# Hybrid recurrence and pooling block: sums of the heads' outputs made by accumulating stores, pool products moved into the ring of weight blocks

## The chip, the cores and the metric

The kernel runs on one core of a Trainium2 chip. The core has a matrix engine (TensorE, PE in the profile, with its weight loads PEld), a vector engine (VectorE, DVE), a scalar engine (ScalarE, ACT), GpSimd (POOL) and a sync engine (SyncE, SP) that here does nothing but issue DMAs. Work memory is SBUF; matmuls write to the banks of PSUM, of 128 x 512 float32 each. Tensors "in DRAM" are in the chip's memory. Each engine takes its instructions strictly in order, and so does each DMA queue's issuer: an instruction that waits holds all behind it on its engine.

The metric is device time in microseconds (us). Before: a median of 1468.33 us over three runs (1466.95 to 1468.78). Beside them stands one profiled execution, from which the rows shown come.

## What is computed

A decoder block over 1024 tokens of width 1024, in float32. Shortened from the reference:

```python
proj = x @ w_in
q, f_pre, i_val, o_gate, pool_v, gate_a, gate_b = jnp.split(proj, splits, axis=-1)
o = hgrn2_chunked(qf, 1 - f, i_val, log(f))          # 8 heads of 128, a gated recurrence over the tokens
o = o * lax.rsqrt(jnp.mean(jnp.square(o), axis=-1, keepdims=True) + RMS_EPS)
o = o.reshape(B, S, hw) * hgrn_norm_g * jax.nn.sigmoid(o_gate)
a = o @ w_a
pooled = causal_multiscale_pool(pool_v)              # trailing means over 2, 4, 8, 16 tokens, minus the token
b = jnp.einsum('bsgc,gcd->bsgd', pooled, w_pool).reshape(B, S, POOL_WIDTH) * pool_scale
mix = (jax.nn.sigmoid(gate_a) * a + jax.nn.sigmoid(gate_b) * b) @ w_out
x = layer_norm(DEEPNORM_ALPHA * x + mix, ln1_g, ln1_b)
x = layer_norm(DEEPNORM_ALPHA * x + jnp.square(jax.nn.relu(x @ w_up)) @ w_down, ln2_g, ln2_b)
```

## The kernel before

**Products.** A float32 matrix product is made of three passes over parts: each operand is split in a high part (an ACT cast, L118 or L123) and a low part (a DVE subtract of source and high part, L119 or L124), and the matmuls take high x high, high x low, low x high. On top of that the large products go by a scheme with seven instead of eight block products. The tokens are the halves u = 0 and 1, the inner dimension is cut in halves as well, and `pair` (L256) makes two column tiles at once: the blocks b11, b12, b21, b22 of the weight are combined by DVE (L273 and the lines of `t4`, L277 to L279), split, and multiplied as P1, P2, P7, P4, P6, P5, P3, in that order, with the token operands a11, a12, s3, a22, s2, s1, s4. Each P is 12 matmuls of 128 x 512 (`prod`, L201 to L204). P1 is copied out of its PSUM bank by ACT (L264), P2 and the others are added by DVE (L268). A pair uses three banks, "a", "c" and "z"; P7 opens "z". A bank comes from the ring of four "pj" or from another tag (w_a's pairs take "hg" and "sc" for "z").

**Rings.** Weight blocks of 256 KB are loaded into "raw" tiles, a ring of six (`block_tile`), in order by SP. Their parts go to "w", a ring of ten tiles, that is five pairs of high and low. Temporary rows lie in "c" (four and two tiles), and in the head stage in q, f (three each), og, v (two each) and others (`tt`, L613).

**Stages.** The values of all heads come first (to about 70 us). Then come eight heads, each in two halves of 512 tokens (`hgrn`, L786): `head_inputs` makes the head's q and f, POOL does small work on the ends of subblocks (L799 on), PE and DVE the recurrence, ACT the squares (L903), a square root (L904) and the scaling (L908), PE turns the result (L911), and DVE multiplies it by the norm's gain and by the gate in the tile og (L912). L913 stores og to `od[h][u]`. The og tile was loaded with the head's gate through `loaded` (L574), on SP.

What is put between the halves as filling is listed in `EXTRAS` (L917 on): `pooled` (w_in's columns for pooling, and the trailing means, stored to `po`), `gates` (w_in's columns of both gates; the gate of b is stored to `gb`), `o_sums`, and `pool_products`.

`o_sums(kp)` (L585) loads the outputs of head kp and head kp+4 in both halves from `od` (four loads), makes the operands s3, s2, s1 and s4 of w_a's seven products with four DVE operations (L588 to L591) and stores them to `osd` (four stores). It runs for kp = 0 to 3, three times as filling and once right after the last half, in tiles tC to tF. `o_operand` loads a11, a12 and a22 from `od`, and s1 to s4 from `osd`, when w_a's pairs need them, and splits them.

`pool_products(g)` loads w_pool's block of group g into a raw tile and splits it, loads the pooled tiles from `po`, splits them, makes four results of six matmuls each (L105 to L107 are the three passes), scales and gates them with `gb` (L709) and stores them to `pb`. All of the parts of w_pool, the pooled tiles and the results come in rotation from the rooms q, f, og and v, twelve in all, so that a room is used again while a store from it may still be under way.

After this come w_a's four pairs (`a_pair`, L981), which add the pooled branch from `pb`, then w_out, the first layer norm, w_up and w_down.

**Order.** The order of instructions on each engine is not the order of the program text: a scheduler sorts them at build time with a timeline of its own (`schedule_with_timeline_sim`), bounded by priorities. So an edit in one place can move instructions elsewhere. PE's order is the same in both kernels up to the sixth head (about 515 us in the profile) and again from the later part of w_a on; in between it differs. The number of matmuls is the same.

Of the kernel before, what the change touches and what calls it, by code (L numbers as in the profile page):

```python
# [9 lines left out]
F32 = mybir.dt.float32  # L10
F32R = mybir.dt.float32r
U32 = mybir.dt.uint32
AF = mybir.ActivationFunctionType
ALU = mybir.AluOpType

_TC = dict(schedule_with_timeline_sim=True)
P = 128
# [4 lines left out]
HEADS = 8  # L22
HALF = 512
CH = HALF // P
# [19 lines left out]
def tile_hybrid_block(  # L44
# [46 lines left out]
    def ps_tile(tag="pj", bufs=4):  # L91
        if tag == "hg":
            hg_tags.append(hg_tags.pop(0))
            tag, bufs = hg_tags[-1], 1
        return pp.tile([P, HALF], F32, tag=tag, name=nm("ps_" + tag), bufs=bufs)
# [20 lines left out]
    def split(src, tile_of):  # L116
        hi, lo = tile_of(), tile_of()
        A.copy(hi, src)  # L118
        V.tensor_sub(lo, src, f(hi))  # L119
        return hi, lo  # L120
# [48 lines left out]

    xt = [[None] * CH for _ in range(3)]  # L170

    def first_tokens(name, *tags):
        for kp in range(CH):
            ps, _ = transposed(r[:CH], HALF if name == "a12" else 0, kp, tags[kp % len(tags)])
            in_parts(name, kp, ps)
            A.copy(xt[name == "a12"][kp], ps)
# [29 lines left out]
    def block_tile(shape=(CH, P)):  # L206
        return wq.tile([P, *shape], F32, tag="raw", name=nm("raw"), bufs=6)
# [45 lines left out]
    def c_late():  # L253
        return c_tile(False)

    def pair(raw, rooms, takes, pz_tag="pj", pc_tag="pj"):  # L256


        b11, b12, b21, b22, t = raw if len(raw) == 5 else (*raw, None)
        c, ps = {}, {}  # L260

        def copied(room, ps):
            t = room()
            A.copy(t, ps)  # L264
            return t

        def added(t, ps):
            V.tensor_add(t, t, ps)  # L268
            return t

        def t3():
            c["t"] = block_tile() if t is None else t
            V.tensor_sub(c["t"], b22, b12)  # L273
            return w_part(c["t"])

        def t4():
            V.tensor_sub(b12, b12, b11)  # L277
            V.tensor_sub(c["t"], b22, b12)
            V.tensor_sub(b21, b21, c["t"])  # L279
            return w_part(b21)  # L280

        def t2():
            return w_part(c["t"])

        def t1():
            return w_part(b12)

        def p1(w):
            ps["a"] = ps_tile()
            prod(ps["a"], w, "a11", True)  # L290
            c[11] = copied(rooms[0], ps["a"])

        def p2(w):
            ps["c"] = ps_tile(pc_tag, 4 if pc_tag == "pj" else 2)
            prod(ps["c"], w, "a12", True)

        def p7(w):
            ps["z"] = ps_tile(pz_tag, 4 if pz_tag == "pj" else 2)
            prod(ps["z"], w, "s3", True)
            with tc.high_priority(PRIO):  # L300
                takes[0](added(c[11], ps["c"]))
                c[22] = copied(rooms[2], ps["z"])

        def p6(w):
            prod(ps["a"], w, "s2", False)
            with tc.high_priority(PRIO):
                c[21] = copied(rooms[1], ps["a"])
                takes[2](added(c[21], ps["z"]))

        def p4(w):  # L310
            prod(ps["z"], w, "a22", False)

        def p5(w):
            prod(ps["a"], w, "s1", False)
            with tc.high_priority(PRIO):
                takes[3](added(c[22], ps["a"]))

        def p3(w):
            prod(ps["a"], w, "s4", False)
            with tc.high_priority(PRIO):  # L320
                takes[1](ps["a"])

        def t0():
            return w_part(b11)

        def b_21():
            return w_part(b21)

        def b_22():
            return w_part(b22)  # L330

        return tuple(
            ((operand,), ((operand, product),))
            for operand, product in ((t0, p1), (b_21, p2), (t3, p7), (t4, p4), (t2, p6), (t1, p5), (b_22, p3))
        )

# [45 lines left out]
    with tc.tile_pool(name="xr", bufs=8, side="right", reuse_waits="tile") as xr:  # L382
# [9 lines left out]
        PE.transpose(ps[:, 0:32], prm_r, ident[0:32, 0:32])  # L392
        V.tensor_copy(prm, ps[:, 0:32])
        g_col, pscale = prm[:, 16:24], prm[:, 24:32]
        lb = const.tile([P, 8], F32, name="lb")
        one_lb = const.tile([P, 8], F32, name="one_lb")
        e01 = const.tile([P, 16], F32, name="e01")
# [174 lines left out]
    def loaded(src, tile_of):  # L572
        t = tile_of()
        nc.sync.dma_start(out=t, in_=src)  # L574
        return t
# [6 lines left out]
            xp[name][kp] = act_tile()  # L582
            split_into(xp[name][kp], loaded(src, c_tile))

    def o_sums(kp, tile_of=c_tile):  # L585

        a11, a21, a12, a22 = (loaded(od[k][u], tile_of) for k, u in ((kp, 0), (kp, 1), (kp + CH, 0), (kp + CH, 1)))
        V.tensor_add(a22, a21, a22)  # L588
        V.tensor_sub(a21, a11, a21)
        V.tensor_sub(a11, a22, a11)  # L590
        V.tensor_sub(a12, a12, a11)  # L591
        for name, t in zip(("s3", "s2", "s1", "s4"), (a21, a11, a22, a12)):
            nc.sync.dma_start(out=osd[name][kp], in_=t)

    hg_scope = ExitStack()
    hgp = hg_scope.enter_context(tc.tile_pool(name="hgp", bufs=1, reuse_waits="tile"))
    mg_scope = ExitStack()
    with tc.tile_pool(name="tmp", bufs=1, side="right", reuse_waits="tile") as tmp:
# [14 lines left out]
        def tt(tag, dtype=F32):  # L613
            pool = tmp if tag in ("q", "f", "og", "v") else hgp
            return pool.tile([P, HALF], dtype, tag=tag, name=nm(tag), bufs=RINGS.get(tag, 1))
# [71 lines left out]

        def pool_products(g):

            tags = iter(("q", "f", "og", "v") * 3)  # L690

            def room(dtype=F32):
                return tt(next(tags), dtype)

            raw = block_tile((2, 2 * P))
            nc.sync.dma_start(out=raw, in_=w_pool[g].rearrange("(k p) c -> p k c", p=P))
            wh, wl = split(raw, lambda: room(F32R).rearrange("p (k c) -> p k c", c=2 * P))
            for u in range(2):
                pl = [split(loaded(pod[2 * g + i][u], room), row_tile) for i in range(2)]
                for i in range(2):  # L700
                    w = slice(i * P, (i + 1) * P)
                    j = 2 * g + i
                    t = room() if j == KT - 1 else loaded(gbd[j][u], room)
                    ps = ps_tile()
                    mm3(ps, [(wh[:, c, w], wl[:, c, w], *pl[c]) for c in range(2)])
                    if j == KT - 1:
                        A.activation(t, ps, AF.Copy, scale=pscale[:, j : j + 1])
                    else:
                        V.scalar_tensor_tensor(t, ps, pscale[:, j : j + 1], t, ALU.mult, ALU.mult)  # L709
                    nc.sync.dma_start(out=pbd[j][u], in_=t)  # L710
# [75 lines left out]
        def hgrn(h, u, ft, q, v, og, state):  # L786
# [122 lines left out]
            pt = ps_tile("tr", 2)  # L909
            for c in range(CH):  # L910
                PE.transpose(pt[:, c * P : (c + 1) * P], on[:, c * P : (c + 1) * P], ident)  # L911
            V.scalar_tensor_tensor(og, pt, g_col[:, h : h + 1], og, ALU.mult, ALU.mult)  # L912
            nc.sync.dma_start(out=od[h][u], in_=og)  # L913
            return st


        EXTRAS = {(h, 1): (("pooled", h),) for h in range(4)}  # L917
        EXTRAS[4, 1] = (("gates", 0),)
        EXTRAS[5, 1] = ("gates", 1), ("o_sums", 0)
        EXTRAS[6, 1] = ("gates", 2), ("o_sums", 1)  # L920
        EXTRAS[7, 0] = (("gates", 3),)
        EXTRAS[7, 1] = (
            ("gates", 4), ("o_sums", 2), ("pool_products", 0), ("gates", 5), ("pool_products", 1), ("gates", 6), ("pool_products", 2), ("pool_products", 3), ("gates", 7),
        )
        nxt = head_inputs(0, (None, None, "p6", None, None, None, None))
        output_gates(0)
        for h in range(HEADS):
            fs, qs = nxt
            state = None
            for u in range(2):  # L930
                v, og = values(h, u), loaded(ogd[h][u], lambda: tt("og"))
                with tc.high_priority(PRIO_LAST) if (h, u) == (HEADS - 1, 1) else nullcontext():
                    state = hgrn(h, u, fs[u], qs[u], v, og, state)
                    if (h, u) == (HEADS - 1, 1):
                        tags = iter(("tD", "tE", "tF", "tC"))
                        o_sums(h - CH, lambda: tt(next(tags)))
                if h + 1 < HEADS and u:
                    nxt = head_inputs(h + 1)
                    if h % 2:
                        output_gates(h + 1)  # L940
                for what, j in EXTRAS.get((h, u), ()):
                    dict(gates=gates, pooled=pooled, pool_products=pool_products, o_sums=o_sums)[what](j)


        hg_scope.close()
# [34 lines left out]

        def a_pair(p):  # L981
            cols = 2 * p * P, (2 * p + 1) * P
            raw = loaded_blocks(w_a, *cols) if p % 2 else wide_blocks(w_a, cols[0], mg_raw)
            room = mg_tile("room", 4)
            takes = [gated(2 * p + i, u, p < 2) for u in range(2) for i in range(2)]
            return pair(raw, (c_tile, room, room), takes, "hg")

        def unpark(*which):
            for u, j in which:
# [388 lines left out]
```

## Time and profile before

| | us |
|---|---|
| median of three runs | 1468.33 |
| lowest and highest | 1466.95, 1468.78 |
| profiled execution, time | 1467.26 |
| profiled execution, span in the trace | 1465.5 |
| PE busy | 1441.2 |
| DVE busy | 1137.4 |
| ACT busy | 756.8 |
| mean granted clock of TensorE | 0.996 |

How to read the rows that follow in the prediction. A row of the groups has a line of the kernel, its engine and operation, what it writes and reads, the count, then busy time and the mean of one in ns, then idle time just before them with what ended it. A row of the timeline begins with start and duration in us, and has in brackets the idle time before and its releaser. A row of the stretches has from and to, the length, then busy time and count for PE, PEld, DVE, ACT and POOL, the granted clock, the DMA engines' busy share and GB/s. A row of the waits says which engine and line waited for which: total us, times, the longest. A row of the DMA issues has the count, KB each, and the median us from issue to landing. "SPq" and "POOLq" are the queues that these engines issue. L1269 is the line of a load that POOL issues late in the kernel.

### The profile page before, as it was taken

To read this page: it belongs to the slowest core of one execution; us is meant where nothing else is said; L and a number is where in the kernel's file an instruction comes from. 1 tells how busy PE (TensorE), PEld (TensorE's weight loads), DVE (VectorE), ACT (ScalarE), POOL (GpSimd) and SP (SyncE) were. 2 spreads that over 40 slices of the span, in tenths; PEclk is the share of its full clock that TensorE was granted. 3 is DMA by queue.
4 is the path that set the end of the run, shared out by engine and by line. 5 is a ranking of instruction groups with operands and counts; after the bars stand their busy time and mean duration, and the time that the engine had idled before them with its cause. 6 is when DMAs were issued, how large, how long until landed. Compare 5 with 4: busy or idle time off the path is not lost.

```text
span 1465.5 us, 20835 instructions
## 1 busy us (share of the span) xinstructions
PE 1441.2 (98%) x7377; PEld 1189.9 (81%) x7377; DVE 1137.4 (78%) x1838; ACT 756.8 (52%) x1383; POOL 56.2 (4%) x244
## 2 busy tenths in 40 slices
PE   8999999999999999999999999999999999999997
PEld 7788888888888877877888877888888888888886
DVE  5968799999997784758985597666666787778877
ACT  5445465665566655545542366555555543333535
POOL 0001001000010010000002100000000100000000
PEclk9999999999999999999999999999999999999999
DMA  7142233223333445997672125444447774445322
GB/s 261 56 144 81 71 113 111 80 93 110 109 95 129 150 153 188 317 306 240 223 238 101 65 94 172 153 153 148 158 143 266 272 273 152 152 134 174 124 72 115
DMA packets 186056, 226.84 MB, mean 155 GB/s; under 512 B 12096, under 2 KB 109920, under 8 KB 185952
## 3 DMA queue, kind: packets, MB, share of 16 engines
q1 hardware_dynamic: 184016, 218.94, 45.0%
q0 software_dynamic: 1152, 4.19, 0.8%
q10 hardware_dynamic: 784, 2.38, 0.5%
q8 instruction: 58, 0.95, 0.3%
q14 instruction: 46, 0.38, 0.1%
HBM read 154.16 MB, written 71.30 MB: 154 GB/s over the span
## 4 chain that ended last, share of the span: by engine, by line
PE 85%; DMA 7%; DVE 5%; issue 1%; ACT 1%; SPq 1%; DVEq 0%; ACTq 0%
PE ps_pj L201 15%; PE ps_pj L203 15%; PE ps_pj L204 15%; PE ps_pj L1260 4%; PE ps_pj L1261 4%; PE ps_pj L1259 4%; DMA raw<-in_w_in_dram 2%; PE ps_pj L105 2%; PE ps_pj L107 2%; PE ps_pj L106 2%; PE ps_tr L1261 1%; PE ps_tr L1260 1%; PE ps_tr L1259 1%; PE ps_hg L204 1%; DMA draw<-in_w_down_dram 1%
## 5 line engine op out<-in xcount | busy, mean ns | idle before, releaser
L201 PE MATMUL ps_pj<-act,w 128*128 128x512 f32 x1068 | 422.9, 397 | 5.2 <-ACT c L264 3.2
L203 PE MATMUL ps_pj<-act,w 128*128 128x512 f32 x1068 | 415.0, 390 | 0.0
L204 PE MATMUL ps_pj<-act,w 128*128 128x512 f32 x1068 | 414.3, 391 | 0.0
L118 ACT CAST w<-raw 128x512 fp32r<-128x512 f32 x311 | 191.7, 622 | 251.1 <-PE ps_pj L203 157.6
L119 DVE TENSOR_TENSOR w<-raw,w 128x512 fp32r<-128x512 f32 x311 | 211.6, 686 | 79.6 <-ACT w L118 76.7
L201 PEld LDWEIGHTS ps_pj<-act,w 128*128 128x128 f32 x1068 | 200.9, 188 | 50.4 <-ACT c L264 3.8
L204 PEld LDWEIGHTS ps_pj<-act,w 128*128 128x128 f32 x1068 | 200.8, 188 | 42.4
L203 PEld LDWEIGHTS ps_pj<-act,w 128*128 128x128 f32 x1068 | 201.1, 188 | 39.9
L1221 ACT CAST act<-act 128x1024 fp32r<-128x1024 f32 x66 | 67.1, 1052 | 109.2 <-PE ps_pj L1260 35.9
L1260 PE MATMUL ps_pj<-act,act 128*128 128x512 f32 x240 | 93.3, 389 | 0.1
L1261 PE MATMUL ps_pj<-act,act 128*128 128x512 f32 x240 | 93.0, 389 | 0.0
L268 DVE TENSOR_TENSOR c<-c,ps_pj 128x512 f32<-128x512 f32 x95 | 64.7, 682 | 35.9 <-PE ps_pj L204 32.7
L1259 PE MATMUL ps_pj<-act,act 128*128 128x512 f32 x240 | 92.4, 389 | 0.0
L1222 DVE TENSOR_TENSOR act<-act,act 128x1024 fp32r<-128x1024 f32 x66 | 79.3, 1220 | 15.2 <-ACT act L1221 15.2
L264 ACT COPY c<-ps_pj 128x512 f32<-128x512 f32 x96 | 55.7, 582 | 11.7 <-PE ps_pj L204 6.2
L797 DVE RECIPROCAL tC<-tA 128x128 f32<-128x128 f32 x64 | 54.4, 907 | 0.0
L1260 PEld LDWEIGHTS ps_pj<-act,act 128*128 128x128 f32 x240 | 45.1, 188 | 9.9 <-DVE act L1222 0.5
L1259 PEld LDWEIGHTS ps_pj<-act,act 128*128 128x128 f32 x240 | 45.0, 188 | 9.4
L1261 PEld LDWEIGHTS ps_pj<-act,act 128*128 128x128 f32 x240 | 45.1, 188 | 9.2
L273 DVE TENSOR_TENSOR raw<-raw,raw 128x512 f32<-128x512 f32 x43 | 29.6, 689 | 26.0 <-DMA raw<-in_w_in_dram 22.5
L1130 ACT ACTIVATE c<-c 128x512 f32<-128x512 f32 x61 | 38.7, 634 | 1.5
L1129 ACT ACTIVATE c<-c 128x512 f32<-128x512 f32 x46 | 29.1, 633 | 15.5 <-DVE c L268 15.5
(413 smaller groups left out, 2656.1 us busy)
## 6 DMA issues: line engine op xcount, KB each, us to landing
h<-c SPq DMA_DIRECT2D x106, 256.0 KB, 2.9
raw<-in_w_in_dram SPq DMA_DIRECT2D x100, 256.0 KB, 3.1
act<-h SPq DMA_DIRECT2D x78, 256.0 KB, 3.0
draw<-in_w_down_dram SPq DMA_DIRECT2D x16, 1024.0 KB, 7.9
raw<-in_w_up_dram SPq DMA_DIRECT2D x56, 256.0 KB, 3.0
hf<-h SPq DMA_DIRECT2D x34, 256.0 KB, 2.8
c<-o SPq DMA_DIRECT2D x24, 256.0 KB, 4.3
v<-v SPq DMA_DIRECT2D x16, 256.0 KB, 3.1
```

Source lines behind the costliest of these rows:

```text
L118: A.copy(hi, src)
L119: V.tensor_sub(lo, src, f(hi))
L201: PE.matmul(ps, wh[:, k], th, start=first and k == 0, stop=False, skip_group_check=True)
L203: PE.matmul(ps, wh[:, k], tl, start=False, stop=False, skip_group_check=True)
L204: PE.matmul(ps, wl[:, k], th, start=False, stop=k == CH - 1, skip_group_check=True)
L264: A.copy(t, ps)
L268: V.tensor_add(t, t, ps)
L1221: A.copy(hi, src)
L1222: V.tensor_sub(lo, src, f(hi))
L1259: PE.matmul(ps, hh[:, w], wh, start=fresh and n == 0, stop=False, skip_group_check=True)
L1260: PE.matmul(ps, hh[:, w], wl, start=False, stop=False, skip_group_check=True)
L1261: PE.matmul(ps, hl[:, w], wh, start=False, stop=n == M - 1, skip_group_check=True)
```

## The change

The heads' outputs are no longer loaded, summed and stored. `put_output` stores each half as it is made: to `od` (except the second halves of heads 0 to 3, which nothing else reads), and directly onto s1 to s4. The first contribution to a sum is a plain store from SP; each later one is a store from POOL that adds to what is in DRAM. Adding allows no subtraction, so the second halves are multiplied with the negative gain `g_neg`, which turns the signs of s2, s1 and a22; `pair(..., turned=True)` turns the weights' combinations of w_a instead. For a second half of heads 0 to 3 there are three adding stores, for heads 4 to 7 one in the first half and three in the second: 28 in all, of 256 KB each.

`pool_products` loads w_pool's block and all four pooled tiles into the ring of weight blocks at its start; the parts of w_pool take q and f, the results take v, c, f, c. The filling after the last half has another order. P7's bank is taken in P2, ahead of P2's own, where it comes from the "pj" ring. In w_a, pairs 0 and 3 load by single blocks, pairs 1 and 2 by wide ones, pair 1 with its b11 once more in a tile of the block ring.

```diff
+    def minus_sum(out, a, b):
+        V.scalar_tensor_tensor(out, a, -1.0, b, ALU.mult, ALU.subtract)
...
-    def pair(raw, rooms, takes, pz_tag="pj", pc_tag="pj"):
+    def pair(raw, rooms, takes, pz_tag="pj", pc_tag="pj", turned=False):
...
         def t4():
-            V.tensor_sub(b12, b12, b11)
-            V.tensor_sub(c["t"], b22, b12)
-            V.tensor_sub(b21, b21, c["t"])
+            if turned:
+                V.tensor_sub(b12, b11, b12)
+                minus_sum(c["t"], b22, b12)
+                minus_sum(b21, c["t"], b21)
+            else:
+                V.tensor_sub(b12, b12, b11)
+                V.tensor_sub(c["t"], b22, b12)
+                V.tensor_sub(b21, b21, c["t"])
             return w_part(b21)
...
         def p2(w):
+            if pz_tag == "pj":
+                ps["z"] = ps_tile()
             ps["c"] = ps_tile(pc_tag, 4 if pc_tag == "pj" else 2)
             prod(ps["c"], w, "a12", True)
 
         def p7(w):
-            ps["z"] = ps_tile(pz_tag, 4 if pz_tag == "pj" else 2)
+            if pz_tag != "pj":
+                ps["z"] = ps_tile(pz_tag, 2)
...
+        g_neg = const.tile([P, 8], F32, name="g_neg")
+        V.tensor_scalar_mul(g_neg, g_col, -1.0)
...
-    def o_sums(kp, tile_of=c_tile):
-
-        a11, a21, a12, a22 = (loaded(od[k][u], tile_of) for k, u in ((kp, 0), (kp, 1), (kp + CH, 0), (kp + CH, 1)))
-        V.tensor_add(a22, a21, a22)
-        V.tensor_sub(a21, a11, a21)
-        V.tensor_sub(a11, a22, a11)
-        V.tensor_sub(a12, a12, a11)
-        for name, t in zip(("s3", "s2", "s1", "s4"), (a21, a11, a22, a12)):
+    FIRST = {(0, 0): ("s3", "s2", "s4"), (0, 1): ("s1",), (1, 0): (), (1, 1): ()}
+    ONTO = {(0, 0): (), (0, 1): ("s3", "s2", "s4"), (1, 0): ("s4",), (1, 1): ("s2", "s1", "s4")}
+
+    def put_output(h, u, t):
+
+        right, kp = divmod(h, CH)
+        if (right, u) != (0, 1):
+            nc.sync.dma_start(out=od[h][u], in_=t)
+        for name in FIRST[right, u]:
             nc.sync.dma_start(out=osd[name][kp], in_=t)
+        for name in ONTO[right, u]:
+            nc.gpsimd.dma_start(out=osd[name][kp], in_=t, accum_op=ALU.add)
...
         def pool_products(g):
 
-            tags = iter(("q", "f", "og", "v") * 3)
-
-            def room(dtype=F32):
-                return tt(next(tags), dtype)
-
-            raw = block_tile((2, 2 * P))
-            nc.sync.dma_start(out=raw, in_=w_pool[g].rearrange("(k p) c -> p k c", p=P))
-            wh, wl = split(raw, lambda: room(F32R).rearrange("p (k c) -> p k c", c=2 * P))
+            rooms = iter((lambda: tt("v"), c_tile, lambda: tt("f"), c_tile))
+            raw = loaded(w_pool[g].rearrange("(k p) c -> p k c", p=P), lambda: block_tile((2, 2 * P)))
+            pods = [[loaded(pod[2 * g + i][u], lambda: block_tile((HALF,))) for i in range(2)] for u in range(2)]
+            parts = iter(("q", "f"))
+            wh, wl = split(raw, lambda: tt(next(parts), F32R).rearrange("p (k c) -> p k c", c=2 * P))
             for u in range(2):
-                pl = [split(loaded(pod[2 * g + i][u], room), row_tile) for i in range(2)]
+                pl = [split(pods[u][i], row_tile) for i in range(2)]
                 for i in range(2):
                     w = slice(i * P, (i + 1) * P)
                     j = 2 * g + i
+                    room = next(rooms)
...
-            V.scalar_tensor_tensor(og, pt, g_col[:, h : h + 1], og, ALU.mult, ALU.mult)
-            nc.sync.dma_start(out=od[h][u], in_=og)
+            V.scalar_tensor_tensor(og, pt, (g_neg if u else g_col)[:, h : h + 1], og, ALU.mult, ALU.mult)
+            put_output(h, u, og)
             return st
...
         EXTRAS[4, 1] = (("gates", 0),)
-        EXTRAS[5, 1] = ("gates", 1), ("o_sums", 0)
-        EXTRAS[6, 1] = ("gates", 2), ("o_sums", 1)
+        EXTRAS[5, 1] = (("gates", 1),)
+        EXTRAS[6, 1] = (("gates", 2),)
         EXTRAS[7, 0] = (("gates", 3),)
         EXTRAS[7, 1] = (
-            ("gates", 4), ("o_sums", 2), ("pool_products", 0), ("gates", 5), ("pool_products", 1), ("gates", 6), ("pool_products", 2), ("pool_products", 3), ("gates", 7),
+            ("gates", 4), ("gates", 5), ("pool_products", 0), ("pool_products", 1), ("gates", 6),
+            ("pool_products", 2), ("pool_products", 3), ("gates", 7),
         )
...
-                    if (h, u) == (HEADS - 1, 1):
-                        tags = iter(("tD", "tE", "tF", "tC"))
-                        o_sums(h - CH, lambda: tt(next(tags)))
...
         def a_pair(p):
             cols = 2 * p * P, (2 * p + 1) * P
-            raw = loaded_blocks(w_a, *cols) if p % 2 else wide_blocks(w_a, cols[0], mg_raw)
+            raw = loaded_blocks(w_a, *cols) if p in (0, 3) else wide_blocks(w_a, cols[0], mg_raw)
+            if p == 1:
+                raw[0], _ = wide_block(w_a, 0, cols[0], block_tile())
...
-            return pair(raw, (c_tile, room, room), takes, "hg")
+            return pair(raw, (c_tile, room, room), takes, "hg", turned=True)
```

2 lines of the change are left out of this document (1 added, 1 removed).

## The prediction

> **What bounds the kernel now.** I read the page's busy shares first, then its chain of waits, then the engines' busy time by stretches of 20 us over the part of the span that the change touches, and last the timeline at the stretches where TensorE (PE) is not full.
>
> ```profile
> span 1465.5 us, 20835 instructions
> PE 1441.2 (98%) x7377; PEld 1189.9 (81%) x7377; DVE 1137.4 (78%) x1838; ACT 756.8 (52%) x1383; POOL 56.2 (4%) x244
> PE 85%; DMA 7%; DVE 5%; issue 1%; ACT 1%; SPq 1%; DVEq 0%; ACTq 0%
> ```
>
> PE is busy for 1441.2 of 1465.5 us, and the chain that ends last runs over PE for 85%. The change removes and adds no matmul. So it can only gain inside the 24.3 us in which PE stands still, plus time in which PE runs at a lower clock, and it can lose whatever new waits it puts on PE. Where the idle time lies:
>
> ```profile
> core 0: us, PE busy (x) PEld busy (x) DVE busy (x) ACT busy (x) POOL busy (x), PEclk, DMA share, GB/s
> 90.00:520.00 430.00, 430.00 (x2758) 357.12 (x2757) 373.48 (x724) 255.14 (x563) 32.97 (x186) 1.00 0.33 103
> ...
> 540.00:560.00 20.00, 18.86 (x139) 14.81 (x138) 19.96 (x39) 13.39 (x26) 1.65 (x10) 1.00 0.69 226
> 560.00:580.00 20.00, 17.20 (x78) 13.85 (x77) 4.51 (x8) 8.76 (x22) 0.00 (x0) 0.91 0.52 172
> 580.00:600.00 20.00, 20.00 (x103) 16.93 (x102) 16.44 (x29) 14.24 (x32) 0.00 (x0) 1.00 0.88 293
> 600.00:620.00 20.00, 19.68 (x87) 15.95 (x87) 14.27 (x23) 7.33 (x13) 0.00 (x0) 1.00 0.93 300
> 620.00:640.00 20.00, 20.00 (x89) 16.30 (x88) 10.79 (x17) 9.18 (x16) 0.00 (x0) 1.00 0.92 316
> 640.00:660.00 20.00, 17.04 (x68) 13.55 (x67) 12.95 (x22) 10.77 (x20) 0.00 (x0) 0.91 0.91 299
> ...
> 680.00:700.00 20.00, 19.09 (x82) 14.89 (x80) 15.85 (x26) 11.91 (x22) 0.00 (x0) 1.00 0.99 342
> 700.00:720.00 20.00, 19.85 (x87) 16.44 (x88) 19.53 (x33) 8.44 (x16) 0.00 (x0) 1.00 0.59 193
> ```
>
> From 90 to 520 us, through seven heads, PE has no gap at all: whatever the change does for a head there gains nothing. From 540 to 720 us the rows lack 1.14 + 2.80 + 0.32 + 2.96 + 0.91 + 0.15 = 8.28 us, and in two of them the granted clock is 0.91. This is the stretch of the last head, the gates and the pool products, whose order the change rewrites. The rest of the 24.3 us lies at the start, after 860 us and at the end, where both programs issue the same.
>
> The first large stall is at 570 us:
>
> ```profile
> 566.29 0.39 PE L898 MATMUL ps_hg<-st,tA 128*128 128x128 f32 x2
> 570.20 0.33 PE L911 MATMUL ps_tr<-ident,tH 128*128 128x128 f32 x1 [0.74 <-ACT tH L908]
> 573.36 0.50 PE L201 MATMUL ps_pj<-act,w 128*128 128x512 f32 x1 [2.06 <-ACT c L264]
> 567.94 1.28 ACT L904 ACT_TABLE_LOAD   x1
> 570.94 1.28 ACT L676 ACT_TABLE_LOAD   x1
> 572.72 1.07 ACT L264 COPY c<-ps_pj 128x512 f32<-128x512 f32 x2
> 574.00:577.30 3.30, 3.30 (x9) 2.57 (x8) 0.00 (x0) 0.18 (x1) 0.00 (x0) 0.50 0.50 176
> ```
>
> PE stands for 0.74 us on the last half's scaled output (L908), then for 2.06 us on a copy out of PSUM (L264) of gate pair 4. The copy comes so late because ACT does the normalisation with its two function-table loads of 1.28 us ahead of it. Then the clock is 0.50 for 3.30 us, which loses half of that, 1.65 us. The stall costs 0.74 + 2.06 + 1.65 = 4.45 us. The second is at 641 us:
>
> ```profile
> 643.94 0.62 ACT L118 CAST q<-raw 128x512 fp32r<-128x512 f32 x1 [3.95 <-DMA pb<-q]
> 644.62 0.50 PE L105 MATMUL ps_pj<-w,q 128*128 128x512 f32 x1 [2.96 <-ACT q L118]
> 645.70:649.00 3.30, 3.30 (x9) 2.68 (x9) 3.00 (x6) 1.43 (x3) 0.00 (x0) 0.50 0.97 316
> ```
>
> Here the cast of a pool product's weight waits 3.95 us for its room, which the store of an earlier product to pb still holds; PE waits 2.96 us for the cast and loses 1.65 us to the clock: 4.61 us.
>
> **The change part by part.** *Pool products.* In the new order w_pool and the pooled tiles go into the block ring, ahead of time, and the weight's parts take q and f alone, while results take v, c, f, c. The cast at 643.94 then no longer waits for a store to pb from its own room: its wait falls away, −4.61 us. What is late next is DVE's subtract of the low part (0.686 us in L119's row below), which stands in the new order well ahead of these matmuls. The new list puts pool_products 1 right behind pool_products 0, with gates 6 after them. In the instructions as they will be issued, the 24 matmuls of product 1 stand in a row on four PSUM banks.
>
> ```profile
> L119 DVE TENSOR_TENSOR w<-raw,w 128x512 fp32r<-128x512 f32 x311 | 211.6, 686 | 79.6 <-ACT w L118 76.7
> L709 DVE SCALAR_TENSOR_TENSOR q<-ps_pj,prm,q 128x512 f32<-128x512 f32 x8 | 5.9, 743 | 1.7 <-DMA q<-gb 1.7
> L273 DVE TENSOR_TENSOR raw<-raw,raw 128x512 f32<-128x512 f32 x43 | 29.6, 689 | 26.0 <-DMA raw<-in_w_in_dram 22.5 <-issue 1.8 <-DMA raw<-in_w_up_dram 1.4
> ```
>
> At 0.225 us each (89 in the 20.00 us of the row 620 to 640) they take 5.4 us. DVE must meanwhile do four subtracts (4 × 0.686) and four products (4 × 0.743), 5.7 us, and gates 6 needs a free bank right behind. Bounds for this spot: 0, if DVE is ahead, to two DVE operations late, 1.4 us. I take 1.0. Some smaller waits of the new order (a bank, a load of gb with 1.7 us of idle DVE before L709 in the row above) I put at 0.5, between 0 and 1.7.
>
> *The stall at 570 us.* In the new order gate pair 4's copy stands ahead of the normalisation on ACT, and the first transpose of the last half stands 38 matmuls (8.6 us) behind the last matmul that the normalisation needs. In the old trace that chain took from 566.29 (matmul L898) to 570.20, 3.9 us; the cast of w_pool's weight now stands in it too, and can wait for its load. There is room of some 4 us, so I take the whole stall as gone: −4.45. What it costs if the cast's load comes late: the stall again, up to 4.45.
>
> *The stall at 544 us* (1.14 us) has the cast of w_pool ahead of the copy that PE waits for:
>
> ```profile
> 544.30 0.62 ACT L118 CAST q<-raw 128x512 fp32r<-128x512 f32 x1 [0.77 <-DMA raw<-in_w_pool_dram]
> 544.83 0.58 ACT L264 COPY c<-ps_pj 128x512 f32<-128x512 f32 x1
> ```
>
> That cast moves back and takes its 0.77 + 0.62 us along, but a second table load (1.28 us) and the scaling of L908 (1.14 us) now stand before the copy. Bounds −1.14 to +1.28; as the two nearly cancel, I take 0.
>
> *o_sums removed.* 16 loads, 16 DVE operations and 16 stores go.
>
> ```profile
> L590 DVE TENSOR_TENSOR c<-c,c 128x512 f32<-128x512 f32 x3 | 2.1, 688 | 0.0
> L590 DVE TENSOR_TENSOR tD<-tC,tD 128x512 f32<-128x512 f32 x1 | 0.7, 691 | 0.0
> ```
>
> Sixteen of 0.69 us are 11 us of DVE, hidden behind PE except in the row 600 to 620, where the last four stand before the operation that PE waits 0.32 us for: −0.32. The last half's outputs were loaded, summed and stored again before w_a's operands could be read; now accumulating stores finish earlier than that. The stalls of 0.91 and 0.15 us at 680 to 720 stand on ACT casts and PSUM banks as before: 0, bounds −1.06 to +1.0.
>
> *Accumulating stores.* Of 44 stores onto the four sums, 16 go out from SP as plain stores, 28 from POOL with an add; four of the 16 stores of outputs fall away. The trace has no accumulating DMA. The nearest rows:
>
> ```profile
> L1269 POOL DMA_DIRECT2D act<-x x7 | 3.9, 559 | 332.7 <-PE ps_pj L204 332.1
> act<-x POOLq DMA_DIRECT2D x7, 512.0 KB, 7.4
> o<-og SPq DMA_DIRECT2D x16, 256.0 KB, 2.2
> SPq L574 <- DMA o<-og: 24.5, 13, 3.9
> POOL T L799 <- DVE tA L791: 223.5, 15, 43.6
> ACT w L118 <- PE ps_pj L203: 85.1, 57, 4.7
> DVE raw L273 <- DMA raw<-in_w_in_dram: 8.9, 9, 3.3
> ```
>
> POOL needs 0.56 us to issue one, 1.7 us for three, and it waits for DVE for 15 us at a time before its next work (223.5/15): hidden. The landing is the unknown. An accumulate of 256 KB reads and writes its target, so it lies between a plain store (2.2 us) and a POOL load of 512 KB (7.4 us); three at once take 2.2 us if they overlap, 22.2 us if they run one after the other. I take 8, about one of 512 KB. What waits is SP: the next half's gate output goes into the ring of two og tiles, so its load stands in SP's queue until the last reader of the tile has landed, as now for the plain store (24.5 us in 13 waits, at most 3.9). Behind it stand the weight blocks. At 8 us SP is held 5.8 us longer per second half. Cover: w's ring holds five pairs of parts, each worth 12 matmuls, so 5 × 12 × 0.225 = 13.5 us of PE work, and ACT is stopped by a full ring 57 times in 90 to 520 us. So 0 on the path, and from 13.5 us on every microsecond counts.
>
> The Trainium skill ("DMA: Bandwidth & Descriptors", section "Anatomy of one DMA — SWDGE (gpsimd) path") fits a DMA issued from GpSimd at 2.0 us plus bytes over 436e3, which is 2.6 us for 256 KB, an estimate of 7.8 us for three in a row; the trace's 7.4 us for 512 KB against its 3.2 shows that it holds only without traffic beside. By the fit, too, the sum would get 0 here.
>
> *The rest.* The turned signs make two of the operations of a w_a pair 0.743 instead of 0.689 us: 8 × 0.054 = 0.4 us of DVE, which is 15.85 busy of 20 there: 0, at most 0.4. P7's bank taken before P2's changes nothing while no PE wait on a bank shows in the heads (90 to 520 us): 0.
>
> Sum: −4.61 − 4.45 − 0.32 + 1.0 + 0.5 = −7.9 us. The profiled execution of before took 1467.26 us (span 1465.5 and 1.8 around it), so 1459.4. The median of the runs shown, 1468.33, is 1.1 above that execution, so 1460.4; I say 1460.
>
> **The rivals.** *A: the sums hold SP back, slower.* Place: SP's queue at each next load into og, seven second halves. Point: three accumulates above 2.2 + 13.5 = 15.7 us. For it: the serial price of 22.2 us passes that, and DVE waits for a block 9 times already. Against: six loaded blocks lie ahead as well, and the queues move on average only 0.33 of their share there. Each half is 6.5 us late, and the clock takes 1.65 us more; in three of the seven, 24.5 us, less 7.9: 1468.3 + 16.6 = 1485.
>
> The Trainium skill ("SBUF — State Buffer", "A bandwidth-pool intuition that's wrong (but worth ruling out)") warns of this: a GpSimd DMA took about 3.1 instead of 0.62 us beside certain VectorE copies, because its descriptors could not be written. An estimate by it is 2.5 us more per store, 7.5 for three, still under the point; no run here shows it.
>
> *B: the pool products fill the block ring.* Each takes five tiles of the ring of six from the gate weights. From 520 to 720 us:
>
> ```profile
> DVE raw L273 <- DMA raw<-in_w_in_dram: 13.6, 4, 5.7
> ACT w L118 <- DMA og<-po: 11.6, 4, 4.7
> ```
>
> DVE waits for a gate block up to 5.7 us there. For it: transfers take 0.9 of their share from 580 to 660. Against: the loads of sums leave that stretch, and the old waits for po (11.6 us) go. One such wait reaching PE with the clock's 1.65 is 7.35 us: the gain is used up, 1467.8. Two: 1475.
>
> *C: one of the two big stalls stays* (the normalisation's chain, or a room still late): 1468.3 − 7.9 + 4.5 = 1465.
>
> *D: all of the stretch goes*, 8.28 + 3.30 = 11.6 us, with nothing new: 1456.7.
>
> **How the numbers follow.** Forecast 0.42, own range 1457 to 1464 (the bounds at 544, at 1.4 + 1.7 for the new order and at ±1 for the last two stalls, not all at once); D 0.10; C 0.12, half of it faster; B with one wait 0.09, with two 0.14; A 0.13. About 0.2%, 2.9 us, is what a measurement of this kernel can tell from no change. Faster: 0.42 + 0.10 + 0.06 = 0.58; same 0.06 + 0.09 = 0.15; slower 0.14 + 0.13 = 0.27. The range 1455 to 1476 leaves out A and little else.
>
> **What would show it.** Right: PE without a gap over 1 us and at clock 1.00 from 560 to 660 us; no ACT wait for a pb store; small waits of 1 to 2 us on PSUM banks in product 1. Accumulates landing in about 3 to 8 us, SP's wait before og under 10 us, PE still full from 90 to 520. Wrong: a gap in that first stretch (A); gate blocks late by more than 5 us, or clock below 1.00 between 600 and 700 us (B); the copy of gate pair 4 again behind the table loads (C).

## The result, and the profile after

The changed kernel took 1486.92 us, a median of four runs from 1486.34 to 1487.48, against 1467.64 for the kernel before in the same comparison: a ratio of 1.0131, 95% interval 1.0113 to 1.0149. It is slower by 19 us, where 1460 was forecast; the range ended at 1476. The number lies beside that of rival A (1485), but A's mechanism did not happen: that the sum of a wrong rival came out near is chance, and the trace tells them apart at once.

The page of the profiled execution (span, busy shares, chain), and from its groups the first matmul of each triple (L204):

```profile
span 1485.6 us, 20853 instructions
PE 1463.3 (98%) x7377; PEld 1189.6 (80%) x7377; DVE 1132.1 (76%) x1823; ACT 757.5 (51%) x1383; POOL 80.7 (5%) x272
PE 95%; DMA 2%; DVE 1%; ACT 1%; issue 0%; SPq 0%; DVEq 0%; ACTq 0%
L204 PE MATMUL ps_pj<-act,w 128*128 128x512 f32 x1068 | 427.9, 401 | 1.8 <-ACT w L118 1.3
```

The same group in the kernel before (there L201):

```profile
L201 PE MATMUL ps_pj<-act,w 128*128 128x512 f32 x1068 | 422.9, 397 | 5.2 <-ACT c L264 3.2 <-ACT w L118 0.6 <-ACT act L123 0.5
```

The span grew by 20.1 us and PE's busy time by 22.1 (1441.2 before), with the same 7377 matmuls. PE does not wait longer: 1485.6 − 1463.3 = 22.3 us idle against 24.3. The matmuls themselves take longer. The group has a mean of 401 instead of 397 ns, and the stretches say where:

```profile
90.00:520.00 430.00, 430.00 (x2717) 349.73 (x2716) 366.21 (x711) 245.17 (x545) 48.55 (x196) 1.00 0.42 117
540.00:560.00 20.00, 20.00 (x144) 16.25 (x143) 16.70 (x31) 12.20 (x31) 2.00 (x10) 1.00 0.43 132
560.00:580.00 20.00, 20.00 (x152) 16.57 (x152) 12.46 (x23) 9.20 (x16) 2.66 (x3) 1.00 0.69 168
580.00:600.00 20.00, 20.00 (x94) 16.33 (x93) 10.62 (x19) 13.88 (x31) 0.86 (x1) 1.00 0.58 174
600.00:620.00 20.00, 20.00 (x99) 16.55 (x98) 9.39 (x16) 12.78 (x29) 2.62 (x3) 1.00 0.64 188
620.00:640.00 20.00, 14.81 (x54) 11.15 (x53) 11.50 (x18) 5.32 (x10) 0.00 (x0) 0.83 1.07 369
640.00:660.00 20.00, 20.00 (x88) 16.21 (x87) 10.96 (x17) 9.56 (x18) 0.00 (x0) 1.00 0.79 262
680.00:700.00 20.00, 19.46 (x83) 15.01 (x81) 15.44 (x25) 11.14 (x20) 0.00 (x0) 1.00 0.71 221
700.00:720.00 20.00, 19.20 (x81) 15.11 (x82) 18.73 (x31) 11.54 (x21) 0.00 (x0) 1.00 0.99 343
900.00:1000.00 100.00, 100.00 (x430) 80.31 (x430) 66.17 (x104) 57.52 (x98) 0.00 (x0) 1.00 0.49 163
1200.00:1300.00 100.00, 100.00 (x443) 82.84 (x442) 81.27 (x89) 37.51 (x38) 0.00 (x0) 1.00 0.53 182
```

The same two stretches of w_up (900 to 1000) and w_down (1200 to 1300) in the kernel before:

```profile
900.00:1000.00 100.00, 100.00 (x443) 82.83 (x442) 62.37 (x96) 56.06 (x95) 0.00 (x0) 1.00 0.45 150
1200.00:1300.00 100.00, 99.91 (x441) 82.41 (x440) 77.28 (x85) 35.27 (x36) 0.00 (x0) 1.00 0.43 142
```

In w_up both programs do the same operations, PE is busy all the time, the granted clock is 1.00 in both, and yet 100 us hold 430 matmuls instead of 443. In the heads, 2717 instead of 2758 fit in 430 us, from the first head on, long before any sum is stored. In w_down the pace is as before. Taken over all starts of matmuls of 512 columns in the trace (intervals of 200 to 260 ns), the median is 234 instead of 227 ns up to w_up's end, and what lies above 226.7 ns adds up to 26.6 us instead of 1.9. This sum is called the pace lost below; it moves by about half a microsecond with where the intervals are cut off. So 24.7 us go to a slower pace of PE, more than the 20.1 by which the span grew; all the rest is 4.6 us better.

That rest has the gains of the forecast and one larger loss. From 540 to 620 us and from 640 to 660 PE is full at clock 1.00, where the stalls at 544, 570, 612 and 641 us were. In place of them there is one at 622 us. The timeline of PE and DVE there:

```profile
627.08 0.79 PE L105 MATMUL ps_pj<-w,q 128*128 128x512 f32 x1 [4.71 <-DVE c L723]
625.07 0.69 DVE L276 TENSOR_TENSOR raw<-raw,raw 128x512 f32<-128x512 f32 x1 [4.63 <-DMA raw<-in_w_in_dram]
626.28 0.75 DVE L723 SCALAR_TENSOR_TENSOR c<-ps_pj,prm,c 128x512 f32<-128x512 f32 x1
```

Product 1 waits for a bank that DVE empties with L723. Ahead of that on DVE stands L276, the first combination of gate pair 6, and waits 4.63 us for a block of w_in. The clock of the row 620 to 640 is 0.83. It is at half for 6.8 us, which begin while PE still stands:

```profile
625.80:632.60 6.80, 5.04 (x11) 3.57 (x12) 6.73 (x11) 1.76 (x3) 0.00 (x0) 0.50 1.06 386
```

PE works for 5.04 us of them, so the half clock costs 2.5 us, and the whole stall 4.71 + 2.5 = 7.2 us.

### The profile page after: what moved, and what is told of

Same layout as the page of the kernel before. It is cut to its first block, busy times and chain, and to the rows that moved or that the text cites. A ratio compares the mean times of both kernels' runs of the same rounds, so it can differ in the third digit from the quotient of the medians.

```text
span 1485.6 us, 20853 instructions
## 1 busy us (share of the span) xinstructions
PE 1463.3 (98%) x7377; PEld 1189.6 (80%) x7377; DVE 1132.1 (76%) x1823; ACT 757.5 (51%) x1383; POOL 80.7 (5%) x272
## 4 chain that ended last, share of the span: by engine, by line
PE 95%; DMA 2%; DVE 1%; ACT 1%; issue 0%; SPq 0%; DVEq 0%; ACTq 0%
PE ps_pj L204 17%; PE ps_pj L207 16%; PE ps_pj L206 16%; PE ps_pj L1275 4%; PE ps_pj L1273 4%; PE ps_pj L1274 4%; PE ps_pj L105 2%; PE ps_pj L106 2%; PE ps_pj L107 2%; PE ps_tr L1275 1%; PE ps_tr L1273 1%; PE ps_tr L1274 1%; PE ps_hg L207 1%; PE ps_hg L204 1%; PE ps_sc L204 1%; PE ps_sc L207 1%
## 5 line engine op out<-in xcount | busy, mean ns | idle before, releaser
L204 PE MATMUL ps_pj<-act,w 128*128 128x512 f32 x1068 | 427.9, 401 | 1.8 <-ACT w L118 1.3
L206 PE MATMUL ps_pj<-act,w 128*128 128x512 f32 x1068 | 421.4, 395 | 0.0
L207 PE MATMUL ps_pj<-act,w 128*128 128x512 f32 x1068 | 419.5, 396 | 0.0
L118 ACT CAST w<-raw 128x512 fp32r<-128x512 f32 x327 | 201.6, 620 | 311.3 <-PE ps_pj L206 188.7
L119 DVE TENSOR_TENSOR w<-raw,w 128x512 fp32r<-128x512 f32 x327 | 222.8, 688 | 102.7 <-ACT w L118 101.0
L204 PEld LDWEIGHTS ps_pj<-act,w 128*128 128x128 f32 x1068 | 200.6, 188 | 51.0 <-ACT w L118 2.9
L276 DVE TENSOR_TENSOR raw<-raw,raw 128x512 f32<-128x512 f32 x43 | 29.7, 690 | 23.2 <-DMA raw<-in_w_in_dram 20.4
```

The lines of the kernel that those rows point to most:

```text
L204: PE.matmul(ps, wh[:, k], th, start=first and k == 0, stop=False, skip_group_check=True)
L206: PE.matmul(ps, wh[:, k], tl, start=False, stop=False, skip_group_check=True)
L207: PE.matmul(ps, wl[:, k], th, start=False, stop=k == CH - 1, skip_group_check=True)
```

## The experiments

What came new at the very start of the program is `g_neg`, a tile of 32 bytes in each partition, among the constants at the lower end of SBUF. The act tiles lie behind it and moved up by 32 bytes; the tiles of w are placed from the upper end and stayed. In w_down both operands come from act. A line, below, is a multiple of 64 bytes in SBUF. Three theories came from this: the place of the operands in SBUF (1), the accumulating stores and POOL's work (2), and for the stall at 622 us the block ring (B).

**The column made 64 bytes wide.** The order on every engine stays that of the changed kernel.

```diff
-        g_neg = const.tile([P, 8], F32, name="g_neg")
+        g_neg = const.tile([P, LINE], F32, name="g_neg")[:, :8]
```

> The changed kernel with g_neg in 64 bytes of a partition instead of 32, so that all tiles behind it lie where they lay before; the order on every engine is that of the changed kernel. Theory 1 (the place in SBUF: the new 32 byte column shifts the tiles of act against those of w by 32 bytes, and each matmul that takes one operand from each is 6 to 7 ns slower): the matmuls start 227 ns apart again, 24.7 us come back (26.6 us over 226.7 ns in the changed kernel's trace, 1.9 in that of before), 1462. Theory 2 (the accumulating stores, or the work on POOL for them, slow PE through the memory): nothing of that is touched, 1487 and 234 ns.

1474.55 us (1473.02 to 1475.49), 1.0045 of before (1.0028 to 1.0062). About two thirds of the loss came back, with all stores in place. The row of w_up:

```profile
900.00:1000.00 100.00, 100.00 (x438) 82.05 (x437) 64.37 (x99) 55.76 (x95) 0.00 (x0) 1.00 0.52 172
```

438 matmuls, neither 430 nor 443; 12.3 us of pace are left. Theory 2 falls as the cause, and theory 1 in its simple form (a line of 64 bytes) as well: act is now 64 bytes off, on its line, and it still costs. So being on a line or off it does not decide.

**The column alone, in the kernel before.**

```diff
+        G.memset(const.tile([P, 8], F32, name="shift"), 0.0)
         lb = const.tile([P, 8], F32, name="lb")
```

> The kernel before with an unused column of 32 bytes in front of lb, as g_neg lies in the changed kernel, and nothing else. Theory 1: 234 instead of 227 ns from the first values to the end of w_up, +24.7 us, 1492. Theory 2: unchanged, 1468.

1488.49 us (1487.05 to 1490.08), 1.0142 (1.0120 to 1.0164), 26.6 us of pace, the same as in the changed kernel. The row of w_up (its PE was idle for 0.35 us):

```profile
900.00:1000.00 100.00, 99.65 (x427) 80.09 (x428) 64.60 (x100) 56.47 (x97) 0.00 (x0) 1.00 0.46 156
```

Thirty-two unused bytes make the whole loss, without one line of the change.

**Both sides moved, in opposite directions.** The changed kernel with a longer pad at the upper end, which moves w down by 32 bytes while g_neg moves act up by 32.

```diff
-    G.memset(pad.tile([P, 24], F32, name="pad_top"), 0.0)
+    G.memset(pad.tile([P, 32], F32, name="pad_top"), 0.0)
```

> The changed kernel with the 32 byte g_neg, and the pad at the upper end of SBUF 32 bytes longer, so that w and all tiles of the right side are shifted by 32 bytes like act on the left. Theory 1a (what counts is that the two operands differ in their place in 64 bytes; w_down, with both operands in shifted act tiles, ran at 227 ns): 227 ns, 1462. Theory 1b (any operand that is off its 64 bytes is slow): 234 ns, 1487 or more. Theory 2: 1487.

1475.59 us (1473.13 to 1476.81), 1.0049 (1.0030 to 1.0068), 12.5 us of pace:

```profile
900.00:1000.00 100.00, 100.00 (x439) 82.05 (x438) 63.38 (x97) 55.50 (x95) 0.00 (x0) 1.00 0.49 163
```

I had taken "both shifted" as no difference between them; since w moved down, they are 64 bytes apart, as in the run with the wide column, and the pace is the same. Neither form of the theory gave the number, but the two runs agree in the distance and in nothing else: here both stand off a line of 64, there both on it.

**Both sides moved together.** The changed kernel, act and w both up by 32 bytes.

```diff
-    G.memset(pad.tile([P, 24], F32, name="pad_top"), 0.0)
+    G.memset(pad.tile([P, 16], F32, name="pad_top"), 0.0)
```

> The changed kernel with g_neg in 32 bytes and the pad at the upper end 32 bytes shorter, so that the tiles of w move up by the same 32 bytes as those of act: both stand off a line of 64 bytes, by the same amount, 0 apart modulo 512 as in the kernel before (e1_line and e3_both_shift had them 64 apart and kept 12.3 and 12.5 us of the slower pace). Theory 1a in its full form (what counts is the distance of the two operands, not the place of either): 227 ns, under 2 us of pace left, 1464. If 64 bytes of absolute place counted: 231 to 234 ns, 1475 to 1487. The stall at 614 us (5.6 us, and 6.8 us at half clock) stays.

1467.30 us (1464.01 to 1470.72), 0.9990 of before (0.9977 to 1.0003), 1.6 us of pace:

```profile
900.00:1000.00 100.00, 100.00 (x443) 82.81 (x442) 62.01 (x96) 56.67 (x97) 0.00 (x0) 1.00 0.46 151
```

443 matmuls again, though both operands begin 32 bytes off a line: the distance counts, not the place. The change without its accident is neutral. It came 3 us above the expectation of 1464, which is just below the fastest of its ten runs. The stall is there, somewhat longer than in the changed kernel:

```profile
614.76 0.69 DVE L276 TENSOR_TENSOR raw<-raw,raw 128x512 f32<-128x512 f32 x1 [5.64 <-DMA raw<-in_w_in_dram]
616.77 0.79 PE L105 MATMUL ps_pj<-w,q 128*128 128x512 f32 x1 [5.72 <-DVE c L723]
SPq L587 <- DMA s<-og: 55.3, 16, 7.7
SPq L695 <- ACT c L692: 6.8, 2, 6.4
```

(The last two rows are waits of SP's queue, from 90 to 720 us and from 585 to 625 us.)

**Other engines.** One rival is that the moved tiles bring DVE, ACT or the DMAs in the way of PE's reads. No run was made for it, but the traces tell. From 900 to 1100 us, 80 intervals between starts of matmuls in the changed kernel lie wholly in idle time of DVE, ACT and POOL, and their mean is 233.5 ns; 180 lie wholly in work of both DVE and ACT, with 233.2. In the kernel before there are 83 and 164 of them, and both have 226.7. With no DMA under way either, 13 have 233.4 against 21 of 226.8. So the slower pace needs no other engine.

**Other distances**, with the unused column in the kernel before, of 128 and of 256 bytes; one run each.

> The kernel before with an unused column of 128 bytes in front of lb: act 128 bytes from where it lay against w, both on a line of 64. So far 0 apart gave 1.6 to 2.0 us of pace, 32 apart 26.6, 64 apart 12.1 to 12.5. If the pattern repeats after 128 bytes: 227 ns and under 2 us. If the pace falls off with the distance (26.6, 12.3 and so on): 6 us. If any distance but 0 costs as much as 64: 12 us.

1487.57 us, 24.1 us of pace.

```profile
900.00:1000.00 100.00, 100.00 (x432) 81.07 (x431) 64.72 (x100) 57.01 (x98) 0.00 (x0) 1.00 0.49 163
```

> The same with 256 bytes. If the pattern repeats after 128 or 256 bytes: under 2 us of pace. If any distance but 0 modulo 512 costs: 3 to 12 us.

1467.19 us, 1.9 us of pace.

```profile
900.00:1000.00 100.00, 100.00 (x443) 82.81 (x442) 62.38 (x96) 55.84 (x94) 0.00 (x0) 1.00 0.45 149
```

The distance of 128 misses all three guesses; 256 is as good as none.

**The sums alone.** Accumulating stores, signs, no o_sums; pool products, P7's bank, filling order and w_a's loads as before. First with the wide column (64 apart), then 0 apart, as above.

> The accumulating stores, the signs and the removal of o_sums alone, with g_neg in 64 bytes; pool products, P7's bank, the order of the filling (without o_sums) and w_a's loads as before. Theory 1: 227 ns; the stall of the pool products at 641 us is left (4.6 us), that at 570 us may go: 1460 to 1468. Theory 2: 234 ns from the first stores on, 1480 to 1490.

1480.52 us (1474.14 to 1481.09), 1.0077 (1.0051 to 1.0102), with 12.1 us of pace: slower than theory 1 had it, and in the range of theory 2. But w_up, with 439 matmuls, has the pace of 64 apart again and not 234 ns, so the time alone misleads; the next run takes the distance away.

> The accumulating stores, the signs and the removal of o_sums alone (as e4_sums_only), with the operands 0 apart. Theory 1a: the 10 us of pace that e4_sums_only had go, 1470. If the accumulating stores cost PE something by themselves: 1475 or more. It shows what the stores do without the pool products' part.

1468.64 us (1465.55 to 1474.18), 1.0007 (0.9990 to 1.0023). The pace is that of before, and so is the time:

```profile
900.00:1000.00 100.00, 100.00 (x443) 82.81 (x442) 62.14 (x96) 55.26 (x94) 0.00 (x0) 1.00 0.47 155
```

The stores do not slow the matmuls, and the stores and the removal of o_sums together change nothing that can be measured. What each of the two does by itself was not run.

**The pool products alone.** The kernel before with the new `pool_products` and the new filling order, o_sums kept.

> The kernel before with the changed pool products and the changed order of the filling (o_sums 2 kept, behind gates 4); sums, P7's bank and w_a's loads as before; no new column, so the operands lie as before. Theory B (the pool products fill the block ring, so gate 6's blocks come late and DVE stands in front of product 1): the stall of 5 us with half clock behind it is there, the wait for pb at 641 us is gone, so 1464 to 1470. Theory S (that stall comes from the accumulating stores' traffic): no such stall, 1460 or less.

1472.48 us (1470.21 to 1475.41), 1.0026 (1.0011 to 1.0041): above both theories. PE's waits from 540 to 720 us, and two operations that stand ahead of them on ACT and DVE:

```profile
PE ps_tr L909 <- ACT tH L906: 2.1, 2, 1.1
PE ps_pj L201 <- ACT c L676: 2.1, 1, 2.1
PE ps_pj L105 <- ACT c L676: 2.1, 1, 2.1
PE ps_pj L105 <- DVE v L707: 1.8, 1, 1.8
569.99 0.63 ACT L118 CAST q<-raw 128x512 fp32r<-128x512 f32 x1 [3.77 <-DMA raw<-in_w_pool_dram]
622.18 0.69 DVE L273 TENSOR_TENSOR raw<-raw,raw 128x512 f32<-128x512 f32 x1 [3.14 <-DMA raw<-in_w_in_dram]
```

Product 1's stall is there, but of 1.8 us only, and by the same chain: L273, the line that is L276 in the changed kernel, waits 3.14 us for a block of w_in, and L707, which empties the bank, stands behind it on DVE. This kernel has no accumulating store, so the chain does not need one. That speaks for theory B, although the time fits neither. The larger losses are two stalls behind the normalisation on ACT (at 572 and 596 us), the old one of 570 us among them, each with 6.8 us at half clock. Ahead of the first the cast of w_pool's weight waits 3.77 us for its load, which the prediction had named as what brings this stall back. The run also shows that in this stretch a part alone does not have the order, nor the stalls, that it has in the whole.

**The order of the filling.** 0 apart, all of the change, but the order of before:

```diff
-            ("gates", 4), ("gates", 5), ("pool_products", 0), ("pool_products", 1), ("gates", 6),
+            ("gates", 4), ("pool_products", 0), ("gates", 5), ("pool_products", 1), ("gates", 6),
```

> The changed kernel with the operands 0 apart and the filling in the order of before (gates 4, pool 0, gates 5, pool 1, gates 6, pool 2, pool 3, gates 7). Theory B: with a gate pair between pool 0 and pool 1 the ring is not filled by ten tiles at once, the stall at 614 us goes with its half clock: 9 us better than e5_rel0, 1455. If the stall comes from SP, which stood 6.4 us on the store of gate 5 before that, it stays or moves: 1460 to 1466.

1462.89 us (1459.74 to 1467.30), 0.9968 (0.9953 to 0.9984). The stall at 611 us is gone, but the time is 8 us above the 1455 of theory B. In the profiled execution, the slowest of the ten, there is another stall, where a weight cast on ACT stands behind loads of w_a's operands:

```profile
688.73 0.79 PE L204 MATMUL ps_pj<-act,w 128*128 128x512 f32 x1 [3.92 <-ACT w L118]
```

And only gate 6 and product 1 exchanged:

```diff
-            ("gates", 4), ("gates", 5), ("pool_products", 0), ("pool_products", 1), ("gates", 6),
-            ("pool_products", 2), ("pool_products", 3), ("gates", 7),
+            ("gates", 4), ("gates", 5), ("pool_products", 0), ("gates", 6), ("pool_products", 1),
+            ("pool_products", 2), ("pool_products", 3), ("gates", 7),
```

> The changed kernel with the operands 0 apart and only gate 6 and pool 1 exchanged (gates 4, gates 5, pool 0, gates 6, pool 1, pool 2, pool 3, gates 7). Theory B (ten tiles of the ring in a row make gate 6's blocks late at product 1): the stall of 5.9 us at 611 us goes, 1460 to 1463; if it is SP's stand on gate 5's store: it stays, 1467.

1462.86 us (1461.70 to 1463.90), 0.9951 (0.9936 to 0.9966). Rows of its SP waits (585 to 625 us) and stretches:

```profile
SPq L695 <- ACT c L692: 8.8, 3, 6.2
600.00:620.00 20.00, 19.90 (x89) 15.89 (x88) 12.98 (x21) 8.37 (x15) 2.62 (x3) 1.00 0.98 301
```

SP stands as long on a gate's store as in the run 0 apart (6.2 and 6.4 us at the longest), and the stall is gone all the same, with the time that theory B had. So it comes from the order of the list, in which two products stand ahead of gate 6. That the ten tiles they take of the ring are what makes gate 6's blocks late fits this, but was not separated from the other moves that the order brings on DVE and SP.

**w_a's loads as before**, in the kernel of the order of before:

```diff
-            raw = loaded_blocks(w_a, *cols) if p in (0, 3) else wide_blocks(w_a, cols[0], mg_raw)
-            if p == 1:
-                raw[0], _ = wide_block(w_a, 0, cols[0], block_tile())
+            raw = loaded_blocks(w_a, *cols) if p % 2 else wide_blocks(w_a, cols[0], mg_raw)
```

> e8_order_rel0 (operands 0 apart, filling in the order of before) with w_a's loads as before the change. That kernel's trace has a stall of 4.1 us at 684 us with half clock behind it, on a weight cast that stands on ACT behind loads of the sums. If the new w_a loads cause it (SP stood 4.9 us on a w_a block there): the stall goes, 1456 to 1460. If the loads of the accumulated sums come late for another reason: it stays, 1463.

1459.04 us (1456.31 to 1461.33), 0.9926 of before (0.9901 to 0.9951): the best of all versions, 28 us below the changed kernel. The page of its profiled execution, the fastest of the four, and the stretch of the stall:

```profile
span 1454.6 us, 20853 instructions
PE 1436.4 (99%) x7377; PEld 1187.6 (82%) x7377; DVE 1127.0 (77%) x1823; ACT 757.2 (52%) x1383; POOL 81.8 (6%) x272
680.00:700.00 20.00, 19.38 (x85) 15.38 (x83) 18.25 (x30) 10.27 (x20) 0.00 (x0) 1.00 1.05 366
```

18.2 us of PE idle time are left, and no stretch of 20 us from 540 to 720 lacks as much as 1 us.

## Why the prediction was wrong

**The step that failed** is the first one: "The change removes and adds no matmul. So it can only gain inside the 24.3 us in which PE stands still, plus time in which PE runs at a lower clock, and it can lose whatever new waits it puts on PE." A third way was left out: each of the matmuls can take longer at full clock. Measured: 24.7 us up to w_up's end, from 32 bytes of constant. `g_neg` was in the diff, was described ahead of the prediction, and had no term in the sum; as an operation it costs one small multiply, and as an allocation it moved every tile of act. None of the rivals had it. With the operands 0 apart the change takes 1467.30 us, so 7 us of the miss remain; product 1's stall, below, costs about as much more than its term.

**The waits that were to go** went: the wait for pb (4.61 forecast), the normalisation (4.45) and the last sums (0.32) leave full rows in the stretches from 560 to 620 and 640 to 660. (The normalisation at 570 us is that of the last head's first half, not of the last half, as the prediction has it; the second follows at 590 us.) The wait at 544 us, put at 0, went too (1.14).

**Product 1** was found as the place of a new wait and mis-sized: 1.0 was taken, from 0 to 1.4, by the DVE operations around it. What came is 4.71 us of standing and 2.5 us by the half clock, 7.2 together. The term should have had the load behind L276, not DVE's own work: DVE takes its instructions in order, and the operation ahead of the bank's release waits for a DMA. That is rival B, with one wait (7.35 us), which had "the gain is used up, 1467.8": 0 apart, the stall is one of 5.72 us with about 2 by the half clock, and the whole change gives 1467.30.

**The accumulating stores** were right as to their effect and nearly so in size:

```profile
s<-og POOLq DMA_DIRECT2D x28, 256.0 KB, 6.4
SPq L587 <- DMA s<-og: 56.8, 15, 8.6
L609 POOL DMA_DIRECT2D s<-og x28 | 24.9, 1149 | 102.3 <-DVE og L926 90.6 <-DVE q L852 7.5 <-DVE k L854 4.2
```

A store lands after 6.4 us (between 2.2 and 7.4, as bounded), and SP waits at most 8.6 us for the tile (8 was taken for three stores), under the 13.5 us of cover. PE is full from 90 to 520 us, so rival A is refuted, although its 1485 is the nearest number. On POOL one costs 1.15 us, not 0.56, in gaps that hold it. That a DMA issued from POOL takes long because of other traffic, as the prediction reads the 7.4 us, no run shows.

**P7's bank and the turned signs** were taken as 0 and not tried by themselves. **w_a's loads** had no price either; in the kernel of the order of before, taking the new loads back is what separates 0.9968 from 0.9926, two ratios from different comparisons whose intervals lie close together (0.9953 and 0.9951). PE's clock also fell to half at the start in this execution (from 11.4 to 18.2 us) and not in that of before, and after 20 us it is 2.9 us behind. The trace of the wide column does not have it, with the same order of instructions; why it comes and goes was not followed.

## What to carry to other kernels

An edit that allocates anything moves what lies behind it: where an engine's busy time grows with an unchanged count of instructions at full clock, compare the matmuls per 100 us in a stage that the edit does not touch, before looking for a wait. Keep the distance of a matmul's two operands when a constant is added, by making up for it in a pad as in the run 0 apart, and test with an unused tile in the old kernel. And a wait on a bank is priced by what stands ahead of the releasing instruction on its engine, its loads included.

## What the runs showed of the hardware

PE's pace depends on the distance in SBUF between the two operands of its matmuls (here w's and act's tiles, in float32, with 512 columns), not on the place of either, as the two placements at 0 and the two at 64 show. Matmuls in the 100 us of w_up, and the pace lost in the whole kernel:

| distance, bytes | matmuls | us of pace | kernels |
|---|---|---|---|
| 0 | 443 | 1.9, 1.6 | before; both moved together |
| 32 | 430, 427 | 26.6, 26.6 | changed; before with 32 bytes |
| 64 | 438, 439 | 12.3, 12.5 | wide column; moved against each other |
| 128 | 432 | 24.1 | before with 128 bytes |
| 256 | 443 | 1.9 | before with 256 bytes |

The loss does not grow or fall steadily with the distance. Within each kernel w's and act's tiles lie at many distances that differ by multiples of 512 bytes, so 0 stands for all of these. One run at 256 is as fast; that the pattern repeats every 256 bytes fits this, but no distance above 256 was run. The distances are those to the placement of the kernel before, in which act and w begin on the same remainder modulo 512. Matmuls that take both operands from act, in w_down, kept 441 and 443 in the two rows shown, with act at 0 and at 32. In w_up of the changed kernel the pace is slower with DVE and ACT idle too (233.5 against 226.7 ns), so what the runs leave is PE's own reads. Which of the two holds the other back stays open: the loads of weights (PEld, busy for 80 of the 100 us) run beside the matmuls, which fill all of them, but no run separated the two.

The Trainium skill ("SBUF — State Buffer", section "Operand start alignment") asks of an operand that it start at a multiple of its element size, as a matter of what is legal and not of speed. All the placements here do so; for the pace, these runs show that it isn't enough.
